# Ten pairs of channel blocks per layer of an input projection made from seven products of quarters instead of eight

## The chip, the cores and the metric

The kernel runs on one core of one Trainium2 chip. The metric is the time of one execution in device microseconds. A core has a matrix engine (PE), a vector engine (DVE), an activation engine (ACT), a general engine (POOL) and a queue engine (SP) that issues the transfers; each works through its own list of instructions in order and waits on semaphores that the others raise. PE writes its sums to PSUM, in banks of 128x512 words.

## What is computed

Two layers of a decoder trunk over 1024 tokens of width 1024. Cut to what matters here, one layer is:

```python
h = rms_norm(x, norm_g)
proj = h @ w_in
(q_lat, kv_lat, k_rope, g_mla,
 c_h, c_b, c_c, g_conv,
 s_q, s_k, s_v, g_swa) = jnp.split(proj, offsets, axis=-1)
y_mla = mla_mixer(q_lat, kv_lat, k_rope, ...) * jax.nn.silu(g_mla)
y_conv = c_b * causal_conv3(c_c * c_h, conv_w) * jax.nn.silu(g_conv)
y_swa = swa_mixer(s_q, s_k, s_v, ...) * jax.nn.silu(g_swa)
return x + jnp.concatenate([y_mla, y_conv, y_swa], axis=-1) @ w_out
```

Three mixers share one input projection `w_in` and one output projection `w_out`: latent attention (`mla`), a short convolution (`conv`) and window attention (`swa`). Each of `c_h`, `c_b`, `c_c` and the three gates `g_` is 512 channels wide, four blocks of 128. These 24 blocks are what the change is about.

## The kernel before

Every matrix product is made in float32 accuracy from two parts: a matrix is split into a rounded part (`hi`) and the rest (`lo`), and `mm3` gives three matmuls for each 128 rows of the sum: hi x hi, hi x lo, lo x hi. The normalised input stands in SBUF transposed, as `xh` and `xl`, for two halves of 512 tokens. A weight chunk comes by DMA into `wraw`; DVE casts it to `whi` (L151) and POOL subtracts to give `wlo` (L153).

A layer runs through these stages.
- **Window stage.** The window attention goes by blocks of 128 tokens. Beside each step, a list (`P1_FILL`) says how many units of the projection PE makes to fill its waits. First come 16 token-major units (`unit_b`, `unit_a`), then channel-major ones: `unit_u` makes `c_h` and `c_c` of a block, `unit_cb` makes `c_b`. Probabilities `pr` are scaled on POOL (L340) ahead of their transposition on PE (L350); `sy` are copies of the transposed ones (ACT L351, DVE L352).
- **Channel-major part.** The rest of the 24 blocks is made by `chan_mm`: for a block of 128 channels and 512 tokens, 8 rows of the sum x 3 matmuls of 128x512, so 24. Two blocks and two halves of the tokens, here called a pair, are 4 x 24 = 96 matmuls. The convolution runs on DVE (L487, L489), a gate is a SiLU on ACT (L400) and a multiplication on POOL (L401). Results stay in SBUF: `ycv` for the convolution, `osw` for the window group, `gm` for the latent group's gate.
- **Output projection of two groups.** `split_y` splits `ycv` and `osw` into `yh` (ACT, L516) and `yl` (DVE and POOL, L517); `unit_o` multiplies by `w_out`. The preparations of the latent attention are spread over these units by lists (`O_STARTS`).
- **Latent attention**, then the output projection of its group and the next layer's input.

Tiles come from pools with a fixed number of buffers (`big` has eight of 2 MB under one tag); whoever asks for a buffer waits until the last use of the one before is over. The order on each engine is that in which the program is written, except where the program asks for an instruction to be put after another.

Of the kernel before, what the change touches and what calls it, by code (L numbers as in the profile page):

```python
# [47 lines left out]
X_BEFORE, X_ALONE, X_FREE = 1, 7, 2  # first input tiles: before the weights, after them, of these without a unit  # L48
P1_ORDER = 'badfe'  # window attention, one step: score, project, transpose, fill, values
P1_FILL = ([0, 0, 2, 1, 0, 1, 1, 2, 1, 2, 0, 0, 2, 1, 0, 1, 0, 2, 0, 1],  # L50
           [2, 2, 2, 2, 0, 0, 3, 1, 2, 1, 1, 2, 0, 1, 0, 1, 1, 2, 3, 0])  # units of the projection beside each step, in the first layer and in the others
C1_STEP, G0_STEP = 3, 16  # steps at which later weights are fetched
O_STARTS = [0, 0, 0, 0, 0, 0, 0, 0, 0, 0, 0, 0, 0, 1, 0, 0, 0, 0, 2, 0, 2, 1, 2, 1, 1, 1, 3, 2, 0, 0, 0, 0]  # attention's preparations per output unit
O_LIGHT = [0, 0, 0, 0, 0, 0, 0, 0, 0, 0, 0, 0, 0, 0, 0, 0, 0, 0, 0, 0, 0, 0, 0, 0, 0, 0, 0, 0, 1, 1, 0, 2]  # attention units per output unit
O_PLAN, O_ALLOC, O_W0 = 28, 10, 7
A_ORDER = 'qk2srsT'  # attention, one step: scores (s), queries (q, r), keys (k, 2), the unit before (T)
A_UNITS = [[0, 3, 1], [0, 3, 0], [1, 0, 0], [0, 2, 0], [1, 0, 1], [0, 2, 1], [1, 1, 0], [1, 1, 1]]  # head pair, query blocks, head
# [11 lines left out]
def trunk(ctx, tc, x, norm_g, w_in, w_qb, w_kvb, w_out, c_gain, c_rope, c_idb, c_ali, out):  # L69
# [13 lines left out]
    wp = ctx.enter_context(tc.tile_pool(name="wp", bufs=2))  # L83
# [48 lines left out]
    x1p = dram.tile([S, D], F32, name="x1p")  # L132
    xmid = dram.tile([S, D], F32, name="xmid")

# [1 line left out]
    def load_w(parts, K, later=None, eng=None):  # L136
        """Two tiles hi, lo [P, K, W]; the pieces run now, or go to the list `later`."""
        W = sum(p.shape[2] for p in parts)
        hi = wp.tile([P, 8 * WMAX], FR, name="whi", tag="hi")[:, :K * W].rearrange("p (k w) -> p k w", k=K)
        lo = wp.tile([P, 8 * WMAX], FR, name="wlo", tag="lo")[:, :K * W].rearrange("p (k w) -> p k w", k=K)  # L140
        st = K // 4

        def piece(k):
            raw = wp.tile([P, 2 * WMAX], F32, name="wraw", tag="raw", bufs=3)
            raw = raw[:, :st * W].rearrange("p (k w) -> p k w", k=st)
            off = 0
            for p in parts:
                w = p.shape[2]
                nc.sync.dma_start(out=raw[:, :, off:off + w], in_=p[:, k:k + st, :])
                off += w  # L150
            v.tensor_copy(hi[:, k:k + st], raw)  # L151
            e = eng[k // st % 2] if isinstance(eng, tuple) else eng or g
            e.tensor_tensor(out=lo[:, k:k + st], in0=raw, in1=f32(hi[:, k:k + st]), op=ALU.subtract)  # L153
# [7 lines left out]
        return hi, lo  # L161
# [60 lines left out]
    for l in range(depth):  # L222
# [649 lines left out]
        for n in range(32):  # L872
# [12 lines left out]
            if lts:  # L885
                lts.pop(0)()
# [116 lines left out]
```

## Time and profile before

| what | value |
|---|---|
| runs | 1594.34, 1597.46, 1597.6 us |
| median | 1597.46 us |
| span of the profiled execution, first to last instruction | 1593.3 us |
| PE, DVE, POOL, ACT busy | 96%, 58%, 47%, 39% |
| window stage, first and second layer | 13 to 247 us, 812 to 1060 us |
| channel-major part | 247 to 459 us, 1060 to 1252 us |
| output projection, with the attention's preparation | 459 to 582 us, 1252 to 1376 us |

The profile records one execution; of that one the span is known, and the table's runs are others. Busy time counts an instruction from start to end; matmuls overlap, so the rate of PE is read from the distance between starts. Stages were cut where the lines of PE's timeline change, to a few microseconds.

### The profile page before, as it was taken

Reading aid. Unit: us, or ns where it says so; the run is one execution under the profiler, and the core shown is the slowest. Engines: PE = TensorE matmul, PEld = TensorE weight load, DVE = VectorE, ACT = ScalarE, POOL = GpSimd, SP = SyncE. Lnnn points to the kernel's source line nnn. Section 1 sums busy time; section 2 is a strip of 40 time slices with the busy share of each in tenths; the row PEclk is TensorE's granted clock in tenths of the full one; section 3 lists DMA queues with packets and bytes.
Section 4 is the critical chain, followed back from the end, with each engine's and each line's share of the span. In section 5 each row is a group of like instructions: output and inputs, shape, how many; then the busy total and the mean of one; then the engine's idle time right before and its main releaser. Section 6 shows DMA issues by size and latency. Waiting matters only on the chain. (4 is left out here: it accounts for less than half of the span.)

```text
span 1593.3 us, 25290 instructions
## 1 busy us (share of the span) xinstructions
PE 1521.6 (96%) x9276; PEld 1340.9 (84%) x9276; DVE 918.6 (58%) x1975; ACT 618.6 (39%) x1583; POOL 742.2 (47%) x976
## 2 busy tenths in 40 slices
PE   6999989999999999999989999989999999999998
PEld 5898868888889988878778988878888899888887
DVE  6676573232136668987656757643221455788864
ACT  4454441000130258985524444310001302688851
POOL 6444252233436646874244443433234466568640
PEclk9999999999999999999999999989999999999999
DMA  6101021122316410012241010121123163100123
GB/s 203 34 1 42 14 54 36 44 53 53 91 51 184 128 48 1 8 60 100 81 128 33 22 35 19 36 53 46 35 52 94 54 195 110 47 2 14 48 75 131
DMA packets 110461, 100.16 MB, mean 63 GB/s; under 512 B 16641, under 2 KB 102529, under 8 KB 110338
## 3 DMA queue, kind: packets, MB, share of 16 engines
q1 hardware_dynamic: 110338, 98.56, 21.0%
q8 instruction: 73, 1.20, 0.3%
q14 instruction: 50, 0.41, 0.1%
HBM read 81.76 MB, written 16.78 MB: 62 GB/s over the span
## 5 line engine op out<-in xcount | busy, mean ns | idle before, releaser
L153 POOL TENSOR_TENSOR wlo<-wraw,whi 128x512 fp32r<-128x512 f32 (+2 forms) x200 | 273.6, 1382 | 276.6 <-DVE whi L151 153.8
L166 PE MATMUL ps_g<-xh,whi 128*128 128x512 f32 x768 | 301.1, 392 | 3.4 <-DVE whi L151 2.2
L151 DVE CAST whi<-wraw 128x512 fp32r<-128x512 f32 (+2 forms) x208 | 136.5, 691 | 289.2 <-PE ps_g L167 199.8
L168 PE MATMUL ps_g<-xh,wlo 128*128 128x512 f32 x768 | 300.4, 391 | 0.3 <-POOL wlo L153 0.3
L167 PE MATMUL ps_g<-xl,whi 128*128 128x512 f32 x768 | 300.0, 391 | 0.0
L166 PEld LDWEIGHTS ps_g<-xh,whi 128*128 128x128 f32 x768 | 144.8, 189 | 34.3 <-issue 1.6
L168 PEld LDWEIGHTS ps_g<-xh,wlo 128*128 128x128 f32 x768 | 144.6, 188 | 30.9 <-POOL wlo L153 0.7
L167 PEld LDWEIGHTS ps_g<-xl,whi 128*128 128x128 f32 x768 | 144.8, 188 | 29.6
L166 PE MATMUL ps_g<-whi,xh 128*128 128x320 f32 (+2 forms) x512 | 157.9, 308 | 3.3 <-ACT xh L192 1.7
L167 PE MATMUL ps_g<-wlo,xh 128*128 128x320 f32 (+2 forms) x512 | 156.0, 305 | 1.7 <-POOL wlo L153 1.7
L168 PE MATMUL ps_g<-whi,xl 128*128 128x320 f32 (+2 forms) x512 | 156.7, 306 | 0.0
L166 PE MATMUL ps_g<-whi,yh 128*128 128x256 f32 x512 | 146.6, 286 | 0.3 <-DVE xr L533 0.3
L167 PE MATMUL ps_g<-wlo,yh 128*128 128x256 f32 x512 | 144.8, 283 | 0.0
L168 PE MATMUL ps_g<-whi,yl 128*128 128x256 f32 x512 | 144.8, 283 | 0.0
L774 PE MATMUL ps_g<-pt,vs 128*128 128x256 f32 (+1 forms) x640 | 120.6, 300 | 13.7 <-DVE pt L769 8.7
L400 ACT ACTIVATE gt<-ps_g 128x512 f32<-128x512 f32 x32 | 19.1, 598 | 250.8 <-PE ps_g L168 250.8
L774 PEld LDWEIGHTS ps_g<-pt,vs 128*128 128x128 f32 x640 | 91.4, 190 | 25.5 <-DVE pt L769 15.1
L769 DVE TENSOR_TENSOR pt<-ps_t,pt 128x512 fp32r<-128x512 f32 (+1 forms) x160 | 100.2, 632 | 16.2 <-ACT pt L768 14.3
L730 PE MATMUL ps_s<-kt,qh 96*128 96x512 f32 (+3 forms) x384 | 106.3, 361 | 1.0
L746 POOL TENSOR_SCALAR apr<-apr,ari 128x896 f32<-128x896 f32 (+2 forms) x80 | 71.7, 896 | 75.3 <-DVE ari L745 63.7
L340 POOL TENSOR_SCALAR pr<-pr,sri 128x256 f32<-128x256 f32 (+1 forms) x128 | 59.1, 480 | 99.7 <-DVE sri L338 62.4
L166 PEld LDWEIGHTS ps_g<-whi,xh 128*128 128x128 f32 x512 | 99.1, 194 | 5.0 <-ACT xh L192 2.3
(197 smaller groups left out, 3473.4 us busy)
## 6 DMA issues: line engine op xcount, KB each, us to landing
wraw<-in_w_out_dram SPq DMA_DIRECT2D x80, 256.0 KB, 3.1
wraw<-in_w_in_dram SPq DMA_DIRECT2D x144, 128.0 KB, 2.3
wraw<-in_w_in_dram SPq DMA_DIRECT2D x56, 256.0 KB, 2.8
x1p<-xr SPq DMA_DIRECT2D x16, 512.0 KB, 3.0
p<-x1p SPq DMA_DIRECT2D x16, 512.0 KB, 3.3
x<-in_x_dram SPq DMA_DIRECT2D x8, 512.0 KB, 4.5
xr<-in_x_dram SPq DMA_DIRECT2D x8, 512.0 KB, 5.3
xmid<-p SPq DMA_DIRECT2D x8, 512.0 KB, 2.8
```

What stands on the lines that cost most here:

```text
L151: v.tensor_copy(hi[:, k:k + st], raw)
L153: e.tensor_tensor(out=lo[:, k:k + st], in0=raw, in1=f32(hi[:, k:k + st]), op=ALU.subtract)
L166: pe.matmul(o, lhsT=lh, rhs=rh, start=(i == 0), stop=False)
L167: pe.matmul(o, lhsT=lh, rhs=rl, start=False, stop=False)
L168: pe.matmul(o, lhsT=ll, rhs=rh, start=False, stop=(i == n - 1))
L340: g.tensor_scalar(out=pr[:, h, k0:], in0=pr[:, h, k0:], scalar1=ri[:, h:h + 1], scalar2=1.0, op0=ALU.mult, op1=ALU.mult)
L400: s.activation(out=gt, in_=o, func=AF.Silu)
L730: pe.matmul(sp[:, kk], lhsT=a[:, hs], rhs=kt[0:QK, b, h, kk], start=(ai == 0), stop=(ai == 2 and c0 + w < n))
L746: g.tensor_scalar(out=pr[:, :n], in0=pr[:, :n], scalar1=ri, scalar2=1.0, op0=ALU.mult, op1=ALU.mult)
L769: v.tensor_tensor(out=pt[:, 1, lo_c:], in0=tp[:, lo_c:], in1=f32(pt[:, 0, lo_c:]), op=ALU.subtract)
L774: pe.matmul(av[:, q0:], lhsT=vb, rhs=pt[:, a, q * 256 + q0:(q + 1) * 256], start=(bb == 0 and bi == 0 and a == 0), stop=(last and bi == 1 ...
```

## The change

The kernel gets a second way to make a pair of blocks. The weights of two blocks of 128 channels are a matrix of two by two quarters (128 channels x 512 rows of the sum), the normalised input one of two by two quarters (512 rows x 512 tokens). Strassen's scheme in Winograd's form gives their product from seven products of quarters instead of eight, each of 4 x 3 = 12 matmuls, with sums of quarters before and after. Per layer:
- Only block 0 of the convolution (`c_h`, `c_c`, `c_b` and its gate) is still made by `chan_mm`, in the window stage and right after it. The other ten pairs go through `seven`, in the order u1, u2, g1, u3, g2, g3, s0, s1, m0, m1 (u: `c_h` and `c_c` of a block; g: `c_b` and the gate of the convolution; s, m: two blocks of the window group's and of the latent group's gate). The second layer's window stage has four units fewer to fill with: 22 instead of 26.
- Sums of the weights are made per pair in `quarters`: four on DVE, seven casts on ACT, the low parts three on DVE and four on POOL.
- Sums of the input's quarters are made once per layer: `t_one` makes T3 and T1 piece by piece in steps 9 to 12 and 14 to 17 of the window stage, `t_rest` makes T2 and then overwrites one quarter of the input itself by the fourth sum (T4), right before the pairs.
- Sums of products: products 1 and 2 gather in PSUM bank a, 6 and 7 in b, then 4 in b, and 5 and then 3 in c. Three banks hold a pair, and two pairs have a set each. ACT copies product 1 (`s1`); DVE makes `s2`, `s3` and the three `plus`, each of which frees a bank for the product behind it.
- SBUF is short for this, so the latents, the window group's output, the convolution's results and the latent group's gate are written to DRAM and read back later. The weight buffers become eight small ones for `hi` and for `lo`. `split_y` moves ahead of the end of this stage, since its inputs come back from DRAM. Three numbers delay the preparation of the latent attention (`O_LAT`, `O_GMR`, `O_ALLOC`).

The core of the diff:

```diff
+        def t_diff(k, tmp, a, b, e):
+            d = tmp()
+            e[0].tensor_tensor(out=d, in0=f32(a[0][:, k]), in1=f32(b[0][:, k]), op=ALU.subtract)
+            e[1].tensor_tensor(out=d, in0=d, in1=f32(a[1][:, k]), op=ALU.add)
+            e[2].tensor_tensor(out=d, in0=d, in1=f32(b[1][:, k]), op=ALU.subtract)
+            return d
...
+        def t_one(n, k):
+            a, b, e = {1: (quarter(0, 1), quarter(0, 0), (g, v, g)), 3: (quarter(1, 1), quarter(0, 1), (g, v, g))}[n]
+            t_split(k, t_diff(k, raw_tile, a, b, e), TT[n][:, 0], TT[n][:, 1])
+
+        def t_rest(k, tmp):
+            f = t_diff(k, tmp, quarter(1, 1), (TT[1][:, 0], TT[1][:, 1]), (v, g, v))
+            t_split(k, f, TT[2][:, 0], TT[2][:, 1])
+            for i in range(2):
+                (v, g)[i].tensor_tensor(out=f, in0=f32(quarter(1, 0)[i][:, k]), in1=f, op=ALU.subtract if i == 0 else ALU.add)
+            t_split(k, f, *quarter(0, 1))
...
+            for n, first in ((3, T_STEPS[0]), (1, T_STEPS[1])):
+                if i == first:
+                    t_alloc(n)
+                if first <= i < first + 4:
+                    with tc.issue_after(marks["exp"].ins):
+                        t_one(n, i - first)
...
+            def split(n, a, e):
+                h, lo = (t.rearrange("p (k c) -> p k c", k=4) for t in w_pair(512))
+                s.copy(out=h, in_=a)
+                e.tensor_tensor(out=lo, in0=a, in1=f32(h), op=ALU.subtract)
...
+            v.tensor_tensor(out=t, in0=a21, in1=a22, op=ALU.add)
+            split(1, a11, g)
+            split(5, t, g)
+            v.tensor_tensor(out=a21, in0=a11, in1=a21, op=ALU.subtract)
+            v.tensor_tensor(out=t, in0=t, in1=a11, op=ALU.subtract)
+            split(6, t, v)
+            split(7, a21, v)
+            split(2, a12, g)
+            v.tensor_tensor(out=t, in0=a12, in1=t, op=ALU.subtract)
+            split(4, a22, g)
+            split(3, t, v)
...
+            a, b, c = ps_c()
+            product(a, 1, True)
+            s1 = st()
+            s.copy(out=s1, in_=a)
+            if first:
+                product(c, 5, True)
+                product(a, 2, False)
+                c11(a)
+            product(b, 6, True)
+            s2 = st()
+            v.tensor_tensor(out=s2, in0=b, in1=s1, op=ALU.add)
+            if not first:
+                product(c, 5, True)
+            product(b, 7, False)
+            s3 = st()
+            v.tensor_tensor(out=s3, in0=b, in1=s1, op=ALU.add)
+            if not first:
+                product(a, 2, False)
+                c11(a)
+            c22(c, s3)
+            product(b, 4, False)
+            c21(b, s1)
+            product(c, 3, False)
+            c12(c, s2)
...
+        w = quarters(O_CH + P, O_CC + P)
+        for k in range(4):
+            t_rest(k, st)
+        osw = a16("osw", F32).rearrange("p (k q) -> p k q", k=4)
+        nc.sync.dma_start(out=osw, in_=osw_d)
+        group_u(1, w)
+        for f, j in ((group_u, 2), (group_g, 1), (group_u, 3), (group_g, 2), (group_g, 3),
+                     (group_s, 0), (group_s, 1), (group_m, 0), (group_m, 1)):
+            f(j)
```

How this changes the order on two engines is shown at two places of the first layer. The names are those of the program with a running number: `st` is a scratch tile, `xh` and `xl` the input's parts, `asum`, `a12` and `wraw` sums or raw weights of a pair.

**POOL at the start of the channel-major part, before.** The rows begin behind the last scaling of probabilities; `ycv` times `gt` is the first block's gate.
```order
L153 TENSOR_TENSOR wlo_2841<-wraw_2842,whi_2840 128x512 [waits DMAHW3_49,DMAHW4_49,DVE_49,PE_49]
L153 TENSOR_TENSOR wlo_2841<-wraw_2847,whi_2840 128x512 [waits DMAHW6_49,DMAHW5_49,DVE_49]
L153 TENSOR_TENSOR wlo_2841<-wraw_2852,whi_2840 128x512 [waits DMAHW7_49,DMAHW0_49,DVE_49]
L153 TENSOR_TENSOR wlo_2841<-wraw_2857,whi_2840 128x512 [waits DMAHW2_49,DMAHW1_49,DVE_49]
L401 TENSOR_TENSOR ycv_2775<-ycv_2775,gt_2809 128x512 [waits DVE_49,Activation_49]
L153 TENSOR_TENSOR wlo_2977<-wraw_2978,whi_2976 128x512 [waits DMAHW3_49,DMAHW4_49,DVE_49,PE_49]
L153 TENSOR_TENSOR wlo_2977<-wraw_2983,whi_2976 128x512 [waits DMAHW6_49,DMAHW5_49,DVE_49]
L401 TENSOR_TENSOR ycv_2775<-ycv_2775,gt_2837 128x512 [waits Activation_49]
```

**POOL at the same place, now.** The first two rows are the last two gate multiplications of block 0.
```order
L537 TENSOR_TENSOR u_2587<-u_2587,ch_2762 128x512 [waits Activation_49]
L537 TENSOR_TENSOR u_2587<-u_2587,ch_2791 128x512 [waits Activation_49]
L472 TENSOR_TENSOR st_2870<-st_2870,xl_331 128x512 [waits DVE_49]
L570 TENSOR_TENSOR wlo_2844<-asum_2837,whi_2843 128x512 [waits Activation_49]
L401 MEMSET u_3010 128x2 [waits DMAHW7_49,DMAHW0_49,Pool_49]
L472 TENSOR_TENSOR st_2880<-st_2880,xl_331 128x512 [waits DVE_49,PE_49]
L472 TENSOR_TENSOR st_2890<-st_2890,xl_331 128x512 [waits DVE_49]
L472 TENSOR_TENSOR st_2900<-st_2900,xl_331 128x512 [waits DVE_49]
L570 TENSOR_TENSOR wlo_2858<-a12_2835,whi_2857 128x512 [waits DMAHW1_49,PE_49,Activation_49]
L570 TENSOR_TENSOR wlo_2863<-wraw_2833,whi_2862 128x512 [waits DMAHW3_49,PE_49,Activation_49]
L487 TENSOR_TENSOR st_2870<-xl_191,st_2870 128x512 [waits DVE_49]
L466 TENSOR_TENSOR T2_2828<-st_2880,T2_2828 128x512 [waits Activation_49]
```

Between the last gate and the low parts of the first pair's weights (`wlo_2844` for product 5, `wlo_2858` for product 2) there now stand sums for T2 and T4 (L472, L487), and eight further rows, sums or low parts, follow until T4's last low part.

**DVE at the end of the channel-major part, before.** The output projection's weights, and the first half of `split_y`.
```order
L151 CAST whi_4017<-wraw_4031 128x512 [waits DMAHW2_49]
L517 TENSOR_TENSOR yl_4036<-ycv_2775,yh_4035 128x512 [waits PE_49,Activation_49]
L517 TENSOR_TENSOR yl_4036<-ycv_2775,yh_4035 128x512 [waits Activation_49] x2
L517 TENSOR_TENSOR yl_4036<-osw_100,yh_4035 128x512 [waits Activation_49] x2
L517 TENSOR_TENSOR yl_4036<-osw_100,yh_4035 128x512 [waits Activation_49,Pool_49]
L151 CAST whi_4140<-wraw_4142 128x512 [waits DMAHW3_49,PE_49,Pool_49]
L151 CAST whi_4140<-wraw_4146 128x512 [waits DMAHW4_49]
```

**DVE at the same place, now.** The second half of `split_y` (L702) stands between the sums of the last pair's products; `ps_c_4214` is the last pair's PSUM, `st` its sums.
```order
L702 TENSOR_TENSOR yl_4346<-yv_4347,yh_4345 128x512 [waits DMAHW1_49,PE_49,Activation_49]
L702 TENSOR_TENSOR yl_4346<-yv_4351,yh_4345 128x512 [waits DMAHW2_49,Activation_49]
L702 TENSOR_TENSOR yl_4346<-yv_4355,yh_4345 128x512 [waits DMAHW4_49,Activation_49]
L702 TENSOR_TENSOR yl_4346<-osw_2910,yh_4345 128x512 [waits Activation_49]
L627 TENSOR_TENSOR st_4267<-ps_c_4214,st_4267 128x512 [waits Activation_49]
L702 TENSOR_TENSOR yl_4346<-osw_2910,yh_4345 128x512 [waits Activation_49]
L702 TENSOR_TENSOR yl_4346<-osw_2910,yh_4345 128x512 [waits Activation_49,Pool_49]
L173 CAST whi_4479<-wraw_4478 128x512 [waits DMAHW6_49,PE_49,Pool_49]
L627 TENSOR_TENSOR st_4227<-ps_c_4214,st_4227 128x512 [waits PE_49]
L173 CAST whi_4485<-wraw_4484 128x512 [waits DMAHW0_49,PE_49]
L627 TENSOR_TENSOR st_4241<-ps_c_4214,st_4241 128x512 [waits PE_49]
```

The `plus` of L627 that frees a bank for product 4 now stands behind four low parts of `yl`, each of which waits for a cast on ACT.

## Rows read from the trace of the kernel before

**Rows 1.** The page's head: busy time and share of the span of each engine.
```profile
span 1593.3 us, 25290 instructions
...
PE 1521.6 (96%) x9276; PEld 1340.9 (84%) x9276; DVE 918.6 (58%) x1975; ACT 618.6 (39%) x1583; POOL 742.2 (47%) x976
```

**Rows 2.** By stage: stretch, length, busy PE, PEld, DVE, ACT, POOL, granted clock, DMA share, GB/s.
```profile
13.00:247.00 234.00, 215.11 (x1394) 193.78 (x1395) 157.92 (x396) 104.85 (x326) 108.44 (x166) 1.00 0.16 43
247.00:459.00 212.00, 212.00 (x937) 175.54 (x936) 53.60 (x70) 16.94 (x28) 74.28 (x57) 1.00 0.22 58
...
812.00:1060.00 248.00, 231.60 (x1439) 210.85 (x1438) 153.24 (x392) 95.05 (x311) 102.60 (x159) 0.96 0.15 38
1060.00:1252.00 192.00, 192.00 (x848) 158.99 (x848) 48.39 (x63) 18.12 (x31) 68.72 (x53) 1.00 0.22 58
```

**Rows 3.** Timeline of PE: start, length; the second row is twelve matmuls after the first.
```profile
439.68 0.39 PE L166 MATMUL ps_g<-xh,whi 128*128 128x512 f32 x1
...
442.40 0.39 PE L166 MATMUL ps_g<-xh,whi 128*128 128x512 f32 x1
```

**Rows 4.** PE's waits by releaser: us in total, times, longest us.
```profile
PE ps_t L350 <- POOL pr L340: 9.9, 6, 4.2
...
PE ps_g L360 <- ACT sy L351: 7.6, 14, 0.6
```

**Rows 5.** Groups by line and shape: busy us, mean ns of one, idle before and releaser.
```profile
L489 DVE SCALAR_TENSOR_TENSOR ycv<-u,gains,ycv 128x512 f32<-128x512 f32 x24 | 21.9, 918 | 0.6
...
L401 POOL TENSOR_TENSOR osw<-osw,gt 128x512 f32<-128x512 f32 x16 | 20.6, 1284 | 28.9 <-ACT gt L400 28.9
...
L400 ACT ACTIVATE gt<-ps_g 128x512 f32<-128x512 f32 x32 | 19.1, 598 | 250.8 <-PE ps_g L168 250.8
...
L516 ACT CAST yh<-ycv 128x512 fp32r<-128x512 f32 x16 | 8.7, 618 | 18.5 <-PE ps_g L167 18.5
...
L388 DVE TENSOR_TENSOR u<-ps_g,ch 128x512 f32<-128x512 f32 x12 | 8.2, 686 | 20.7 <-PE ps_g L168 20.7
...
L487 DVE TENSOR_SCALAR ycv<-u,gains 128x512 f32<-128x512 f32 x12 | 7.3, 621 | 0.4
```

**Rows 6.** Timelines of DVE and then POOL from 453 to 478 us: start, length, count.
```profile
471.75 5.18 DVE L517 TENSOR_TENSOR yl<-ycv,yh 128x512 fp32r<-128x512 f32 x3
...
477.19 0.68 DVE L517 TENSOR_TENSOR yl<-osw,yh 128x512 fp32r<-128x512 f32 x1
...
453.25 1.29 POOL L153 TENSOR_TENSOR wlo<-wraw,whi 128x512 fp32r<-128x512 f32 x1 [0.80 <-DVE whi L151]
...
470.19 4.50 POOL L153 TENSOR_TENSOR wlo<-wraw,whi 128x512 fp32r<-128x512 f32 x3 [4.88 <-PE ps_g L168]
474.64 1.74 POOL L517 TENSOR_TENSOR yl<-ycv,yh 128x512 fp32r<-128x512 f32 x1
```

**Rows 7.** Timeline of PE around 1050 us in the second layer's window stage.
```profile
1047.27 0.69 PE L350 MATMUL ps_t<-idn,pr 128*128 128x128 f32 x2 [4.19 <-POOL pr L340]
...
1051.20 0.63 PE L166 MATMUL ps_g<-xh,whi 128*128 128x512 f32 x1
1051.62 0.63 PE L167 MATMUL ps_g<-xl,whi 128*128 128x512 f32 x1
...
1055.46 0.41 PE L167 MATMUL ps_g<-xl,whi 128*128 128x512 f32 x1
```

**Rows 8.** Stretches around the same place, columns as in rows 2.
```profile
1047.00:1052.00 5.00, 4.22 (x15) 3.59 (x16) 2.09 (x4) 1.07 (x2) 1.57 (x4) 0.50 0.01 2
1052.00:1056.00 4.00, 4.00 (x12) 3.09 (x11) 0.00 (x0) 0.00 (x0) 0.00 (x0) 0.57 0.00 0
1056.00:1060.00 4.00, 4.00 (x19) 3.30 (x18) 0.33 (x1) 1.07 (x3) 0.00 (x0) 1.00 0.00 0
```

**Rows 9.** DMA issues: KB each, median us from issue to landing.
```profile
wraw<-in_w_in_dram SPq DMA_DIRECT2D x144, 128.0 KB, 2.3
```

More of the change, by code (lines that the diff above doesn't have):

```diff
@@ L1 @@
-from contextlib import ExitStack
+from contextlib import ExitStack, nullcontext
 import numpy as np
@@ new lines, in seven, with product @@
+        def seven(c1, c2, c11, c21, c22, c12, w=None):
+            first = w is not None
+            w = w or quarters(c1, c2)
+            def product(o, n, first):
+                (ah, al), (bh, bl) = w[n], qx[n]
+                for k in range(4):
+                    for i, (a, b) in enumerate(((ah, bh), (ah, bl), (al, bh))):
+                        pe.matmul(o, lhsT=a[:, k], rhs=b[:, k], start=(first and k == 0 and i == 0),
+                                  stop=(k == 3 and i == 2), skip_group_check=True)
+            a, b, c = ps_c()
[22 more added lines that the diff above has]
+            c12(c, s2)
@@ new lines, in plus, with silu, group_u @@
+        def plus(o, a):
+            v.tensor_tensor(out=a, in0=o, in1=a, op=ALU.add)
+            return a
+        def silu(o, a=None):
+            r = st() if a is None else plus(o, a)
+            s.activation(out=r, in_=o if a is None else r, func=AF.Silu)
+            return r
+        def group_u(j, w=None):
+            u_tile(j)
+            got = {}
+            seven(O_CH + j * P, O_CC + j * P, lambda o: got.update(a=o),
+                  lambda o, a: v.tensor_tensor(out=uu[j][:, 2:514], in0=got["a"], in1=plus(o, a), op=ALU.mult),
+                  lambda o, a: got.update(d=plus(o, a)),
+                  lambda o, a: g.tensor_tensor(out=uu[j][:, 514:1026], in0=plus(o, a), in1=got["d"], op=ALU.mult), w)
@@ new lines, in group_g, with times, store, last @@
+        def group_g(j):
+            yv = [cp.tile([P, 512], F32, name="yv", tag="yv", bufs=3) for _ in range(2)]
+            for hf in range(2):
+                conv(j, hf, yv[hf])
+            def times(hf, a, e):
+                e.tensor_tensor(out=yv[hf], in0=a, in1=yv[hf], op=ALU.mult)
+            def store(hf):
+                nc.sync.dma_start(out=ycv_d[:, j, hf * 512:hf * 512 + 512], in_=yv[hf])
+            def last(o, a):
+                times(1, plus(o, a), g)
+                store(1)
+            def c21(o, a):
+                times(0, silu(o, a), g)
+                store(0)
+            seven(O_CB + j * P, O_GC + j * P, lambda o: times(0, o, v), c21, lambda o, a: times(1, silu(o, a), g), last)
```

244 lines of the change are left out of this document (148 added, 96 removed).

## The prediction

> **What bounds the kernel now.** I read the page's busy times first: PE is busy 96% of the span and no other engine is above 58% [rows 1]. Because such a share averages unlike stages, I then cut the span at the stages. In the channel-major part PE never stops (212.00 of 212.00 us in the first layer, 192.00 of 192.00 in the second), while DVE, ACT and POOL have 53.60, 16.94 and 74.28 us of work in the first [rows 2]. So there the time is the number of matmuls times the distance between their starts. In the two window stages PE stands still for 18.9 and 16.4 us [rows 2], most of it behind POOL's normalisation `pr` (9.9 us) and ACT's copies `sy` (7.6 us) [rows 4].
>
> The distance is read from starts, not from the 0.39 us of one row, since matmuls overlap: twelve 128x512 matmuls lie between 439.68 and 442.40 us [rows 3], so 2.72 / 12 = 0.2267 us each.
>
> **What is removed.** A pair of blocks takes 7 x 12 = 84 matmuls instead of 4 x 24 = 96, for ten pairs in each of two layers: 240 matmuls, 54.4 us, or 27.2 per layer. They come out of a stage where nothing else limits, so this is lost only to new waits. Those follow, per layer.
>
> **Start of the pairs.** Before, POOL had four low parts of weights per four units here. Now its queue holds, behind the last gate's multiplication, 17 operations of 128x512 up to the last low part of the fourth token quarter, and PE needs that after 82 matmuls (six products and ten more), 18.6 us of work. POOL starts them 2.2 us after the last gate unit ends: the SiLU takes 0.60, the multiplication 1.29 [rows 5], the handovers some 0.3. One operation takes POOL 1.29 alone and DVE 0.68 alone; where both run such operations the trace shows both slow: three of DVE in 5.18 us while POOL goes from three in 4.50 to one in 1.74 [rows 6], so one of each in 1.73 us. DVE's queue here has as many two-input operations, so I take 1.73 for all: 2.2 + 17 x 1.73 = 31.6, minus 18.6, gives 13.0 us of stall. It comes in pieces: product 5 waits for the second of the 17, product 2 for the sixth (until 12.6, PE being ready at 8.4: 4.2 us), product 6 for the ninth and tenth, product 4 for the last two. If they do not hinder one another it is 2.2 + 17 x 1.29 - 18.6 = 5.5. One after the other, 1.29 + 0.68 = 1.97 gives 17.1.
>
> That pair of rows is where a rule bears on the change. The Trainium skill (SBUF — State Buffer, Who interferes with whom) says that a DVE operation with two SBUF inputs and a GpSimd operation that reads SBUF take a shared port pair as an exclusive lock, the second one standing still until the first is through. That is the 1.97: 4.1 us more per layer, and about 1615 in all. The trace agrees that they hinder one another, not that nothing overlaps (1.73, not 1.97).
>
> **End of the pairs.** The last pair has no partner whose products could fill its waits, and before this end had no wait at all. Product 2 waits for `s3` (an eviction from PSUM, 0.69 [rows 5], with handovers 0.9). Product 4 waits for the `plus` that frees its bank, and that stands on DVE behind four `yl` of `split_y(1)`, each waiting for a cast on ACT; the casts start when product 2 ends, because `yh` takes a buffer of the normalised input. So 4 x 0.62 [rows 5] + 0.7 + 0.69 = 3.9 us. Product 3 waits for the next `plus`: 0.7 to 1.3. With a slowed `yl` among them I take 7 (5 to 9).
>
> **Clock.** After PE's 4.19 us gap the granted clock is 0.50 to 0.57 until about 1055 us, that is 1.2 instead of 2.4 GHz, and two matmuls are 0.42 apart instead of 0.23 [rows 7, 8]; the ten from 1051.20 to 1055.46 took 2.0 us too long. My chains hold two gaps of about that size per layer. At the start POOL sets the pace, so a slower PE hides; at the end it does not. I take 2 (0 to 4, both or none).
>
> **Steady pairs.** In three pairs (the second gate pair `s` and both `m`) product 1 of the next pair but one comes one matmul behind product 3, and waits for that bank's `plus`: 0.8 each, 2.4 in all. A pair gives PE 84 x 0.2267 = 19.0 us. In a pair of the convolution's gate DVE has seven weight operations (1.73 each beside POOL, 0.68 alone), two convolutions (four `scalar_tensor_tensor` at 0.92 and two scalings at 0.62 [rows 5]), five evictions and a multiplication (0.69 each): 12.1 + 4.9 + 4.1 = 21.1 us, or 13.8 alone. Fully hindered, three such pairs are late by 6.3. I take 5, between 2 (the handovers alone) and 9.
>
> **Window stage.** Its last steps get 20 POOL operations (26 us), 12 on DVE and 8 casts for two token quarters. The second subtraction of a piece waits on POOL for DVE, and the next `pr` stands behind it, which PE already waits for. Projection units beside it can hide that: then nothing. If half of POOL's time shows, 14 (with one more DVE wait). The 16 to 19 us that PE now loses in a whole stage are nearer to the low end; I take 5, some 0.6 for each of eight pieces.
>
> **Transfers.** Spills and reloads of the latents, the window output, the convolution and the last gate are (1.7 + 3 x 2.1) MB, twice, in two layers: 32 MB. In the pairs the DMA engines are busy for 0.22 now [rows 2], and a 128 KB weight load lands in 2.3 us [rows 9], well ahead of its pair. I take nothing; if the 2 MB reload ahead of the second pair's weights showed, it would hide under the start's stall.
>
> **Sum per layer.** 13.0 + 7 + 2 + 5 + 5 = 32.0 of new waiting against 27.2 saved: 4.8 slower, 9.6 for both. The profiled span is 1593.3; the median of the runs, 1597.46, stands 4.2 above it, which I add: 1593.3 + 9.6 + 4.2 = 1607.1. All low ends (12.5) give 14.7 faster per layer, 1568; all high ends (53) 25.8 slower, 1649.
>
> **Rivals.** (a) *Faster, about 1579*: DVE and POOL hinder each other little, since their queues rarely meet (in the pairs now POOL is busy for 74 of 212 us, DVE for 54). Then the start costs 5.5, the steady pairs 2.4, the window 3, the end 7 and the clock nothing: 17.9 instead of 32, 9.3 faster per layer. The point that decides is how long one of the 17 operations takes: with all else as forecast the sum crosses zero when the start costs 8.2, that is at (8.2 + 18.6 - 2.2) / 17 = 1.45 us. Against it: where the trace has both queues full, none ran at its own pace [rows 6].
> (b) *Clean gain, 1543 to 1560*: PE's sequence is held up only at the end. That needs the token sums before the pairs, and the order of POOL's queue puts 17 of its operations behind the last gate.
> (c) *Much slower, about 1633*: the window's `pr` waits for the whole of a token piece (14 per layer) and the three gate pairs are late on DVE throughout (9): 13 + 7 + 2 + 9 + 14 = 45, 17.8 per layer. For it: `pr` is already PE's longest wait there; against: projection units are left in those steps.
> (d) *No change*: the terms cancel within measurement.
> That the matmuls are not saved is no rival: the program holds 240 fewer of the same shape.
>
> **Chances.** The measurement can tell 0.2% (3.2 us) from no change. The forecast case, slower up to 1625, has 0.34; (c), above that, 0.15; (d) 0.12; (a), 1562 to 1594, 0.31; (b) 0.08. So faster 0.39, same 0.12, slower 0.49. The low end of the range leaves out (b), the high end the worst part of (c): 1562 to 1640. Within the forecast's own case it is 1600 to 1625.
>
> **What would show it.** In the profile after: PE with idle stretches summing to 10 to 14 us in the 32 us behind the last gate unit, released by POOL's `wlo`, `T2` and `xl`; DVE's and POOL's sums of 128x512 at 1.3 to 1.8 us where they meet; at the end of the pairs a gap of about 4 us before product 4, released by DVE, and lower clock right behind it; between, PE over 95% busy; window stages longer by some 5 us. I am wrong if POOL's 17 take under 26 us, if the end's casts are there earlier, or if the window stages do not lengthen.

## The result and the profile after

The changed kernel takes 1648.2 us (median; 1646.07 to 1649.39), the kernel before 1597.53 us in the same comparison: ratio 1.0325, 95% interval 1.0306 to 1.0344. The forecast was 1607 with a range to 1640: the direction was right, the size was not, and the time is outside the range. The profiled span is 1647.3 us.

The page's head, beside [rows 1]: 240 matmuls are gone, and PE is busy for 16 us less in a span that is 54 us longer.

```profile
span 1647.3 us, 25601 instructions
...
PE 1505.8 (91%) x9036; PEld 1315.3 (80%) x9036; DVE 1102.5 (67%) x2179; ACT 725.9 (44%) x1763; POOL 856.3 (52%) x1050
```

The windows of the changed kernel in its first layer (columns as in [rows 2]): window stage, start of the pairs, middle, last hundred us.

```profile
13.00:264.30 251.30, 226.09 (x1412) 204.42 (x1412) 174.51 (x409) 112.41 (x337) 133.31 (x182) 0.96 0.18 53
264.30:300.00 35.70, 23.36 (x80) 16.64 (x81) 28.46 (x25) 11.36 (x21) 27.88 (x19) 0.86 0.34 105
300.00:400.00 100.00, 97.91 (x423) 80.00 (x422) 61.46 (x87) 28.50 (x49) 42.53 (x32) 0.98 0.27 72
400.00:499.60 99.60, 84.41 (x341) 66.31 (x340) 52.16 (x62) 32.90 (x57) 47.62 (x34) 0.93 0.35 108
```

Where PE never stopped before [rows 2], it now makes 80 matmuls in 35.7 us and 341 in 99.6, and the clock is down. The middle is nearly full. I call *lost* the length of a stretch less its matmuls, each at the median distance between starts of its form. By this count the pairs lose in the two layers 18.6 and 19.5 us at the start (17.8 and 18.5 of it from their first matmul on, by which the experiments are counted), 4.4 and 2.6 in the middle and 22.6 and 20.5 in the last hundred us; the window stage loses 11.9 and 8.0 more than before (the second counted, in both kernels, from the first matmul of its layer). That is 54.1 per layer on average; less the 27.2 saved, 26.9, and the spans differ by 54.0 / 2 = 27.0.

PE's waits in the changed kernel by releaser (us in total, times, longest), beside [rows 4]. L598 is a matmul of a product, L604 the copy `s1`, L611 `s2`, L616 `s3`, L627 `plus`; `pr`, L340 before, is L365.

```profile
PE ps_t L375 <- POOL pr L365: 17.4, 10, 3.6
PE ps_c L598 <- DVE st L627: 14.6, 10, 4.5
PE ps_c L598 <- DVE st L611: 13.5, 2, 6.8
PE ps_c L598 <- DVE st L616: 10.9, 4, 3.6
PE ps_c L598 <- ACT st L604: 10.1, 8, 1.5
PE ps_g L385 <- ACT sy L376: 8.9, 15, 0.8
...
PE ps_c L598 <- POOL wlo L570: 4.2, 2, 2.1
```

POOL's low parts, on which the forecast put the start's stall, release 4.2 us here. DVE's sums of products and ACT's copies of product 1 release 49. The two longest are `s2`, once per layer. PE's timeline at the start (start, length, and at the end of a row the idle time ahead and its releaser):

```profile
274.95 0.80 PE L598 MATMUL ps_c<-xh,wlo 128*128 128x512 f32 x1 [2.07 <-POOL wlo L570]
...
291.60 1.22 PE L598 MATMUL ps_c<-T,whi 128*128 128x512 f32 x2 [6.76 <-DVE st L611]
```

DVE in the same stretch:

```profile
282.84 1.77 DVE L487 TENSOR_TENSOR st<-xh,st 128x512 f32<-128x512 f32 x1
...
285.13 1.74 DVE L487 TENSOR_TENSOR st<-xh,st 128x512 f32<-128x512 f32 x1
286.80 1.75 DVE L575 TENSOR_TENSOR asum<-wraw 128x512 f32<-128x512 f32 x1
288.46 1.76 DVE L487 TENSOR_TENSOR st<-xh,st 128x512 f32<-128x512 f32 x1
290.15 0.68 DVE L578 TENSOR_TENSOR wraw<-wraw 128x512 f32<-128x512 f32 x1
290.85 0.69 DVE L611 TENSOR_TENSOR st<-ps_c,st 128x512 f32<-128x512 f32 x1
```

`s2` itself takes 0.69 us. PE had stopped at 284.8 with all of product 6 issued, and `s2` began 6.0 us later; it stood behind the sums for T4 and for the next pair's weights, at 1.75 each beside POOL.

PE's timeline in the last hundred us:

```profile
412.49 0.47 PE L598 MATMUL ps_c<-xh,whi 128*128 128x512 f32 x1 [0.65 <-DVE st L627]
...
419.65 0.74 PE L598 MATMUL ps_c<-T,whi 128*128 128x512 f32 x2 [1.45 <-ACT st L604]
...
480.54 0.80 PE L598 MATMUL ps_c<-xh,whi 128*128 128x512 f32 x1 [3.60 <-DVE st L616]
...
490.53 0.79 PE L598 MATMUL ps_c<-xh,whi 128*128 128x512 f32 x1 [4.50 <-DVE st L627]
...
496.80 0.51 PE L598 MATMUL ps_c<-xh,whi 128*128 128x512 f32 x1 [0.78 <-DVE st L627]
```

The second row is odd: it is product 6, the first into bank b, and it waits for ACT's copy `s1`, which reads bank *a*. The first two waits come three times per layer, 2.1 us each time. Ahead of the third, DVE has six low parts of `split_y(0)` in front of `s3`:

```profile
471.66 4.08 DVE L702 TENSOR_TENSOR yl<-yv,yh 128x512 fp32r<-128x512 f32 x3
475.66 2.95 DVE L702 TENSOR_TENSOR yl<-osw,yh 128x512 fp32r<-128x512 f32 x3
...
479.81 0.68 DVE L616 TENSOR_TENSOR st<-ps_c,st 128x512 f32<-128x512 f32 x1
```

The clock in windows around the start's gap (columns as in [rows 2], the granted clock third from the end):

```profile
288.00:292.00 4.00, 0.40 (x1) 0.40 (x2) 3.97 (x5) 1.76 (x4) 3.37 (x3) 0.53 0.00 0
292.00:296.00 4.00, 4.00 (x12) 3.13 (x12) 0.50 (x1) 0.60 (x1) 4.00 (x3) 0.61 0.02 4
```

And in windows behind the two longer gaps of the end:

```profile
480.50:485.00 4.50, 4.46 (x11) 3.51 (x12) 0.00 (x0) 0.05 (x1) 1.15 (x1) 0.50 0.92 335
...
490.50:495.00 4.50, 4.47 (x11) 3.51 (x12) 1.86 (x2) 1.25 (x2) 2.27 (x2) 0.50 0.49 176
```

Eleven matmuls take the 4.5 us in which twenty would fit. Added up over stretches of 2 us, the time at 1.2 GHz is 23 us in the kernel before and 103 us now.

One sentence ahead of the prediction has to be put right: the order on each engine is not simply that of the program's text. In the trace, products of two pairs stand mixed on PE, and `split_y`'s low parts (L702), written behind the last pair, run on DVE ahead of its evictions.

### The profile page after: what moved, and what is told of

Read it like the earlier page. It is cut to its first block, busy times and chain, and to the rows that moved or that the text cites. A ratio compares the mean times of both kernels' runs of the same rounds, so it can differ in the third digit from the quotient of the medians.

```text
span 1647.3 us, 25601 instructions
## 1 busy us (share of the span) xinstructions
PE 1505.8 (91%) x9036; PEld 1315.3 (80%) x9036; DVE 1102.5 (67%) x2179; ACT 725.9 (44%) x1763; POOL 856.3 (52%) x1050
## 5 line engine op out<-in xcount | busy, mean ns | idle before, releaser
L175 POOL TENSOR_TENSOR wlo<-wraw,whi 128x512 fp32r<-128x512 f32 (+2 forms) x120 | 165.7, 1388 | 136.3 <-DVE whi L173 113.0
L598 PE MATMUL ps_c<-T,whi 128*128 128x512 f32 x480 | 155.2, 403 | 26.5 <-DVE st L611 13.5
L598 PE MATMUL ps_c<-xh,whi 128*128 128x512 f32 x320 | 131.2, 410 | 30.0 <-DVE st L627 14.6
L598 PEld LDWEIGHTS ps_c<-T,whi 128*128 128x128 f32 x480 | 91.8, 193 | 52.7 <-DVE st L611 14.4
L598 PE MATMUL ps_c<-xh,wlo 128*128 128x512 f32 x320 | 129.5, 405 | 4.2 <-POOL wlo L570 4.2
L598 PE MATMUL ps_c<-xl,whi 128*128 128x512 f32 x320 | 129.0, 403 | 0.0
L173 DVE CAST whi<-wraw 128x512 fp32r<-128x512 f32 (+2 forms) x128 | 76.8, 609 | 62.5 <-DMA wraw<-in_w_out_dram 20.6
L598 PEld LDWEIGHTS ps_c<-xh,whi 128*128 128x128 f32 x320 | 62.4, 195 | 52.5 <-DVE st L627 13.3
L932 DVE TENSOR_REDUCE am<-ps_s 128x1 f32<-128x128 f32 (+7 forms) x128 | 95.6, 750 | 9.2 <-PE ps_s L930 7.1
L966 ACT CAST pt<-ps_t 128x512 fp32r<-128x512 f32 (+1 forms) x160 | 85.7, 543 | 35.2 <-PE ps_g L192 17.9
```

The source lines that it names most:

```text
L173: v.tensor_copy(hi, raw)
L175: e.tensor_tensor(out=lo, in0=raw, in1=f32(hi), op=ALU.subtract)
L598: pe.matmul(o, lhsT=a[:, k], rhs=b[:, k], start=(first and k == 0 and i == 0), stop=(k == 3 and i == 2), skip_group_check=True)
L932: v.tensor_reduce(out=m, in_=sp[:, :n], axis=AX.X, op=ALU.max)
L966: s.copy(out=pt[:, 0, lo_c:], in_=tp[:, lo_c:])
```

## The experiments

Ratios are to the kernel before, with 95% intervals; the changed kernel is 1.0325. "Lost" is given for the first layer / the second.

### One suspect at a time

**`split_y`'s low parts moved off DVE.**
```diff
-                (g if k % 4 >= 3 else v).tensor_tensor(out=yl[:, k], in0=src, in1=f32(yh[:, k]), op=ALU.subtract)
+                g.tensor_tensor(out=yl[:, k], in0=src, in1=f32(yh[:, k]), op=ALU.subtract)
```


> All low parts of split_y go to POOL instead of three quarters of them to DVE; nothing else changes. Theory (the end of the pairs is slow because the evictions that free a bank stand on DVE behind split_y's low parts, and the gaps of 3.60 and 4.50 us that this makes lower the clock): the two gaps shrink to about 1 us each, the low clock at 480 to 495 us goes, some 2.7 + 3.5 + 4.8 = 11 us per layer, so about 1626 in place of 1648. Rival (the last pair has no partner, so its chain of evictions and the reloads from DRAM are slow in themselves): the gaps stay within 1 us of what they were, 1644 to 1650.

Measured: 1641.36 us, 1.0283 (1.0263 to 1.0304). The gaps of 3.60 and 4.50 became 1.46 and 3.26, the one of 0.78 became 2.53. The end lost 19.0 / 16.3 instead of 22.6 / 20.5: the queue on DVE is part of it, the smaller part.

**Without T2 and T4.**
```diff
-            f = t_diff(k, tmp, quarter(1, 1), (TT[1][:, 0], TT[1][:, 1]), (v, g, v))
...
+                s.copy(out=TT[2][:, i, k], in_=f32(TT[1][:, i, k]))
```


> The sums T2 and T4 right before the pairs are left out: T2 is filled by eight copies on ACT and the overwritten quarter stays as it is, so the products of these quarters are those of other numbers. Theory (the start of the pairs waits for DVE's and POOL's queues of these sums): of 18.6 us lost there some 15 come back in each layer, about 1618. Rival (the first pair's weights, their transfers and their own low parts hold the start): at most 5 per layer come back, 1638 or more.

Measured: 1633.34, 1.0236 (1.0216 to 1.0255). The start lost 7.8 / 7.8 instead of about 18: ten of it belong to these sums, less than the theory said.

**Without T1 and T3.**
```diff
-            t_split(k, t_diff(k, raw_tile, a, b, e), TT[n][:, 0], TT[n][:, 1])
+            for i in range(2):
+                s.copy(out=TT[n][:, i, k], in_=f32(a[i][:, k]))
```


> The sums T1 and T3 in the window stage are left out: both are filled by copies on ACT of one quarter instead of 20 operations on POOL, 12 on DVE and 8 casts per layer. Theory (these operations stand ahead of the scaling of probabilities): PE's loss in the window stages falls from 53.5 and 39.5 us to the 41.6 and 30.2 of before, so 21 us, about 1627. Rival (the loss comes from the other order of the fill units, the later weights and the spills): the loss stays above 48 and 36, 1640 or more.

Measured: 1644.98, 1.0314 (1.0295 to 1.0332). The window stage lost 7.8 / 6.1 less, but the middle of the pairs 3.0 / 6.6 more, so that the end time hardly moved.

**PE kept at work in the waits**, by 24 matmuls into a spare bank ahead of product 7 of the first pair, and 14 and 16 ahead of products 2 and 4 of the last.
```diff
+                for i in range(n):
+                    r = pe.matmul(f, lhsT=k[0], rhs=k[1], start=(i == 0), stop=(i == n - 1), skip_group_check=True)
```


> Matmuls into a spare bank that nothing reads are put into three waits of PE per layer: 24 before product 7 of the first pair, 14 before product 2 and 16 before product 4 of the last. They are shorter than the gaps that they stand in (5.4 of 6.8, 3.2 of 3.6, 3.6 of 4.5 us at full clock). Theory (the half clock after these gaps costs some 2 us at the start and 5 to 6 at the end of each layer's pairs): clock 1.00 there and 8 us less per layer, about 1633. Rival (the half clock does not come from PE's idleness, or costs nothing since other engines set the pace): within 3 us of 1648, or slower.

Measured: 1645.2, 1.0313 (1.0289 to 1.0338). Time at 1.2 GHz fell from 103 to 68 us. At the end, with the fillers counted as lost, the loss fell by 4.1 / 1.7 us: there the low clock has a price of its own. At the start nothing was won, but this does not show that the clock costs nothing there: product 7 began at 292.60 at full clock, and then, with four operations on weights now ahead of `s3` and `plus` on DVE, PE met a wait that the changed kernel does not have, with lower clock behind it (0.81 from 300.9 to 310).

```profile
301.81 0.50 PE L609 MATMUL ps_c<-xh,whi 128*128 128x512 f32 x1 [3.92 <-DVE st L644]
```

**All low parts of `split_y` on POOL as above, and all of `split_y(1)` behind the last SiLU.**
```diff
+        with tc.issue_after(marks["silu"].ins):
+            split_y(1)
-        split_y(1)
```


> As the first experiment (all low parts of split_y on POOL), and the casts of split_y's second half on ACT are put behind the last pair's last SiLU. The first experiment left gaps of 1.46, 3.26 and 2.53 us: the plus before product 4 now waited for a SiLU that stands on ACT behind four of these casts. Theory (at the end of the pairs PE waits for whatever stands ahead of the evictions, on DVE and on ACT): the gap of 3.26 falls to about 1.5 and the low clock there goes, 3 to 4 us more per layer than in the first experiment, ratio 1.023 against its 1.028. Rival (the last pair's chain is that long in itself): the ratio stays at 1.028.

Measured: 1652.83, 1.035 (1.0316 to 1.0383), slower. PE's timeline at the end:

```profile
483.82 0.50 PE L598 MATMUL ps_c<-xh,whi 128*128 128x512 f32 x1 [1.46 <-DVE st L627]
...
491.05 0.80 PE L598 MATMUL ps_c<-xh,whi 128*128 128x512 f32 x1 [4.22 <-DVE st L627]
```

The wait ahead of product 4 went from 4.50 to 1.46, as meant, but product 3 now waits 4.22, and the output projection loses 8.1 / 10.4 instead of 1.4 / 2.2. The work was put off, not hidden.

**u1 made by `chan_mm`**, four units beside T2 and T4, so nine pairs.
```diff
+            s.copy(out=ch, in_=chan_mm(W["u1"], 0, hf))
+            v.tensor_tensor(out=uu[1][:, 2 + hf * 512:514 + hf * 512], in0=chan_mm(W["u1"], P, hf), in1=ch, op=ALU.mult)
...
-        group_u(1, w)
```


> The pair u1 is made by four plain units again, 96 matmuls instead of 84, right after the window stage and its first units; the sums T2 and T4 run beside it. Nine pairs are left. Theory (the start waits for the queues of these sums, which the plain units cover for 21.8 us): of 18.6 us lost at the start some 4 stay, against 2.7 us of matmuls given back, so 12 per layer, ratio 1.018. Rival (whichever pair comes first stalls, since its weights come late and its own evictions stand behind sums on DVE): at least 12 us stay lost, ratio above 1.028.

Measured: 1640.66, 1.0275 (1.0238 to 1.0312). The start of the pairs lost 3.9 / 3.7, but the stall had moved ahead of it:

```profile
292.84 0.77 PE L597 MATMUL ps_c<-xh,whi 128*128 128x512 f32 x1 [7.31 <-DVE u L682]
```

The plain units' own evictions stand behind T2's and T4's sums on DVE.

**T2 and T4 on DVE alone, T1 and T3 on DVE alone** (two kernels).
```diff
-            f = t_diff(k, tmp, quarter(1, 1), (TT[1][:, 0], TT[1][:, 1]), (v, g, v))
+            f = t_diff(k, tmp, quarter(1, 1), (TT[1][:, 0], TT[1][:, 1]), (v, v, v))
```


> The sums T2 and T4 run on DVE alone: its queue at the start gets 12 operations more, POOL's 12 fewer, nothing is left out. Theory (a two-input operation takes 0.68 us on DVE alone and 1.75 beside one on POOL, so sharing this work between them buys nothing): DVE's 35 operations take about 35 x 0.68 + 5 x 1.05 = 29 us instead of 33 for its present share, and the start loses 4 us less per layer: ratio 1.027. Rival (DVE's operations take 1.1 us on average for other reasons, so 12 more of them take 13 us more): the start loses 9 us or more in addition, ratio above 1.043.

> The sums T1 and T3 in the window stage run on DVE alone; POOL loses 20 operations per layer there and DVE gets them, nothing is left out. Theory (the scaling of probabilities on POOL stands behind these sums): PE's wait for it, 17.4 us now and 9.9 in the kernel before, falls to about 11, ratio 1.028. Rival (any 32 operations more in these steps are too many, and DVE has the longer queue): the wait moves to DVE's copies and evictions, ratio 1.033 or more.

Measured: 1647.34, 1.0322 (1.0295 to 1.0349), and 1650.35, 1.0338 (1.0312 to 1.0364). In the first the start lost 15.1 / 15.8, 2.7 less, though DVE had twelve operations more per layer: most now run at 0.60 to 0.69, since POOL is mostly idle, so two engines that take 1.75 each beside one another gain little here over one. What was won there was lost again elsewhere, most of it in the middle. In the second the waits for `pr` fell from 17.4 to 13.0, and 12.9 of waits for scores on ACT stand beside them, 3.9 before. Which of the two engines makes the sums is not what matters.

### The cause at the end: one PSUM tile for three banks

The odd wait of product 6 for a reader of bank a suggested that waits are kept for a whole tile, and `ps_c` is one tile of three banks.
```diff
-        t = pp["pool"].tile([P, 3 * 512], F32, name="ps_c", tag="C", bufs=2)
-        return [t[:, i * 512:i * 512 + 512] for i in range(3)]
+        return [pp["pool"].tile([P, 512], F32, name=f"ps_c{n}", tag=f"C{n}", bufs=2) for n in "abc"]
```


> The three PSUM banks of a pair become three tiles of their own, so that a product waits only for the eviction of its own bank; in the changed kernel one tile holds all three, and a product waits for the last reader of any of them. Theory (at the end and between the last pairs PE waits for evictions of other banks: 0.65 us before product 1 of the next pair but one, 1.45 before product 6, 4.5 before product 4): the three handovers of 2.1 us go, and product 4 waits for s3 alone; some 10 us less wait and 2 us less of low clock per layer, ratio 1.0175 against 1.0325. Rival (the waits are for the data, whose evictions are queued behind other work on DVE and ACT): the waits only move to the next product, ratio above 1.028.

Measured: 1611.34, 1.0098 (1.0079 to 1.0117). This edit of one function, with the same operations, gives back 36.9 us, more than expected. The windows of the start and the middle: the middle is full, 441 matmuls in 99.5 us, and the start is as it was, 18.2 / 18.9.

```profile
265.00:300.50 35.50, 24.81 (x78) 17.01 (x78) 28.43 (x26) 10.36 (x18) 27.96 (x19) 0.81 0.35 111
300.50:400.00 99.50, 99.50 (x441) 82.39 (x440) 68.77 (x90) 30.56 (x52) 48.85 (x33) 1.00 0.26 71
```

Only what PE waits for at the start has changed: `s2` now holds it for 1.12, and a cast of the next pair's weights for 4.40. That cast waits on ACT for DVE's sum of these weights, which stands in the same queue behind the sums for T4.

```profile
292.00 1.22 PE L597 MATMUL ps_cc<-T,whi 128*128 128x512 f32 x2 [4.40 <-ACT whi L568]
```

The end loses 4.5 / 4.5. Its one gap on PE's timeline stands ahead of product 4:

```profile
472.17 0.79 PE L597 MATMUL ps_cb<-xh,whi 128*128 128x512 f32 x1 [2.68 <-DVE st L615]
```

**On that base: u1 by `chan_mm`, and with it the low parts of `split_y` on POOL** (edits as above).

> As the one before, and the pair u1 by four plain units beside the sums T2 and T4. Theory (start and end are separate losses): the 0.5% that the plain pair gave alone adds up, ratio 1.0125. Rival (a stall saved at the start comes back at the end, since the evictions set the pace of all pairs): as without it, 1.0175 or more.

> As the one before, and all low parts of split_y on POOL. Theory (s3 of the last pair still stands behind these on DVE): the 0.4% that this gave alone adds up, ratio 1.008 or 1.009. Rival (with a bank of its own for each product the queue no longer holds PE, and POOL delays the output weights instead): ratio 1.0125 or more.

Measured: 1599.65, 1.0024 (1.001 to 1.0038), and 1611.18, 1.0105 (1.009 to 1.012). The first gains more than its theory said; the second falls between theory and rival. In it the end loses nothing, and the output projection 12.8 / 12.5. PE's wait there is not for `yl` itself but for `xr`, the eviction that adds the layer's input, whose transfer SP issues behind transfers that wait 5.0 for POOL's `yl` and 2.8 for POOL's `wlo`. The waits of PE and of SP's queue in the first layer, from 471 us:

```profile
PE ps_g L189 <- DVE xr L734: 6.9, 1, 6.9
...
SPq L798 <- POOL yl L705: 5.0, 1, 5.0
SPq L150 <- POOL wlo L174: 2.8, 2, 2.0
```

### The start: order or amount

On the kernel with three PSUM tiles and u1 by `chan_mm`: **T4's sums put behind the plain units' last eviction**, and then **`split_y(0)` behind the `plus` that follows the last pair's `s3`**, and then that **without T1 and T3**.
```diff
+        with tc.issue_after(mul.ins):
+            for k in range(4):
+                t_four(k, fs[k])
...
+        with tc.issue_after(marks["c22"].ins):
+            split_y(0)
```


> As the run with a tile per bank and u1 by plain units; in addition DVE's operations for the fourth token quarter T4 are put behind the eviction of the last plain unit. That run still waited at the start, in one layer 7.2 and in the other 4.6 us, for this eviction, which stood on DVE behind the sums. Theory (the order on DVE, not its amount of work, makes this wait): the waits fall to about 1 us, 5 per layer, ratio 0.996 against 1.0024. Rival (the sums are late anyway and product 4 of the first pair then waits for T4): ratio 1.001 or more.

> As the one before, and DVE's low parts of split_y's first half are put behind the last pair's s3 and the plus that frees the third bank. Theory (product 4 of the last pair waits 2.7 us for s3 behind them, and the clock falls after it): some 4 us more per layer, ratio 0.991. Rival (the output projection then waits for these low parts instead): ratio equal to the one before.

> As the one before, with the sums T1 and T3 of the window stage left out and filled by copies on ACT. In the changed kernel this gave 7 us per layer back in the window stages, and 3 to 7 of them were lost again in the pairs. Theory (those were waits for other banks, and the sums cost 7 us per layer in the window stage): ratio lower by 0.009 than the one before. Rival (the time saved in the window stage returns in the pairs for another reason): lower by at most 0.004.

Measured: 1598.26, 1.0023 (1.001 to 1.0036); 1604.37, 1.0066 (1.0043 to 1.0089); 1592.07, 0.998 (0.9966 to 0.9993). In the first the wait for the eviction is gone and another has come:

```profile
303.95 1.22 PE L599 MATMUL ps_cb<-T,whi 128*128 128x512 f32 x2 [4.75 <-DVE st L612]
```

Both orders cost the same, so it is the amount of sums in this place, not their order. In the second the end lost 1.1 / 0.9 and the output projection 8.8 / 9.4, the third edit by which `yl` comes later and is paid for there. The third prices T1 and T3 at 0.0086 of the time, about 7 us per layer.

### The sums made by PE

The sums of the input's quarters are linear, so PE can make them by matmuls with plus or minus the identity: four of 128x512 per piece, 0.9 us, then a cast on ACT and one subtraction on DVE, in place of three sums (two for T4), a cast and a low part that DVE, POOL and ACT share. First T2 and T4, on the kernel with three PSUM tiles and all ten pairs; then T1 and T3 too.
```diff
+        def t_pe(k, a, b, h, lo):
+            o = ps_g()
+            for i in range(4):
+                pe.matmul(o, lhsT=eye[:, i // 2], rhs=(a, b)[i // 2][i % 2][:, k], start=(i == 0), stop=(i == 3))
+            s.copy(out=h[:, k], in_=o)
+            v.tensor_tensor(out=lo[:, k], in0=o, in1=f32(h[:, k]), op=ALU.subtract)
```


> Three PSUM tiles for the three banks, and the sums T2 and T4 of the input's quarters, at the start of the pairs, are made by PE: per slice four matmuls of 128x512 with plus or minus the identity, then a cast on ACT and one subtraction on DVE. All ten pairs and the whole computation are kept. It adds 32 matmuls, 7.3 us, per layer. Theory (the start is lost to the sums' queue on DVE and POOL): the start, 18.2 and 18.9 us lost with three PSUM tiles, falls to about 10 per layer, 7.3 of it the new matmuls; the rest unchanged: ratio 1.000 (0.996 to 1.004) to the kernel before, 1595 us. Rival (PE still waits for the cast and the subtraction of each slice in turn, some 1.3 us per slice): the start costs as much as with the sums on DVE and POOL, ratio 1.008 to 1.012.

> As the kernel with T2 and T4 made on PE, and T1 and T3, in the window stages, too; a scratch tile of the attention's output has one buffer instead of two to make room. The whole computation is kept. 32 more matmuls, 7.3 us, per layer, in a stage where PE has waits. Theory: the window stage loses its 7 us per layer of waits that leaving T1 and T3 out had shown, and half of the new matmuls lie in PE's own waits: 3 us better per layer than the kernel with T2 and T4 alone, ratio 0.997 (0.993 to 1.001). Rival (the new matmuls show in full, and PE waits for the casts on ACT, which the window's softmax uses too): no gain or worse, ratio 1.000 to 1.006.

Measured: 1588.8, 0.996 (0.9947 to 0.9972), and 1580.46, 0.9916 (0.9901 to 0.9931). Both are faster than the kernel before, each at the good end of its theory or beyond it. The page's head of the second:

```profile
span 1578.0 us, 25771 instructions
...
PE 1499.9 (95%) x9164; PEld 1324.2 (84%) x9164; DVE 1064.7 (67%) x2163; ACT 723.1 (46%) x1763; POOL 765.0 (48%) x986
```

The windows of its starts of the pairs:

```profile
258.00:293.70 35.70, 35.70 (x159) 29.57 (x158) 23.23 (x33) 15.78 (x28) 14.09 (x11) 1.00 0.47 145
...
1041.00:1077.00 36.00, 36.00 (x161) 29.81 (x160) 23.07 (x33) 15.97 (x28) 13.95 (x11) 1.00 0.48 146
```

Its PE's waits for `pr`:

```profile
PE ps_t L377 <- POOL pr L367: 6.0, 5, 2.2
```

The start of the pairs, 80 matmuls in 35.7 us in the changed kernel, holds 159 here at full clock, 32 of them for the sums (7.3 us, about the 7.8 that the start still lost when T2 and T4 were left out): PE works through other products while a piece is cast, so the serial wait that the rival counted does not show. In the window stage the waits for `pr` fall from 17.4 to 6.0 us, and with the clock's share the stage loses 13.3 / 10.6 less than in the changed kernel, its new matmuls not counted. The time at 1.2 GHz is 34 us. Against the changed kernel the losses fall by 23.9 in the window stages, 36.3 at the starts, 7.4 in the middles and 35.8 at the ends, and rise by 5.0 in the output projections: 98.4, less 128 matmuls at 0.2267, 29.0, is 69.4, and the spans differ by 69.3.

## Why the prediction was wrong

The sum was 32.0 us of new waiting per layer; it was 54.1. The saving of 27.2 holds. Term by term, as means of the two layers:

| term | forecast | measured |
|---|---|---|
| start of the pairs | 13.0 (5.5 to 17.1) | 19.0 |
| end of the pairs, with the clock | 7 + 2 | 15.2 |
| steady pairs | 5 (2 to 9) | 3.5 in the middle + 6.3 in handovers = 9.8 |
| window stage | 5 (0 to 14) | 10.0 |
| transfers | 0 | no wait of PE's above is released by one |

**End and steady pairs: the step that failed.** These terms are half of the 22 us by which the sum was short (the start is 6, the window stage 5). The prediction let each product wait for the eviction "that frees its bank". What PE waited for was the last reader of any of the three banks, because they are one tile. That puts a handover of 2.1 us between products three times per layer, where I had 0.8 each. Product 2's wait for `s3` was in the sum, at 0.9; it was 3.60, since I had not seen that `s3` reads another bank than the one that product 2 writes, nor that six low parts of `split_y(0)` stand ahead of it on DVE. The 4.50 ahead of product 4 and the 0.78 ahead of product 3 are what was worked out (3.9 and 0.7 to 1.3). With a tile for each bank the end and the steady pairs together cost 4.4 instead of 25.0 per layer. The program's order had shown one name, `ps_c_4214`, on all three `plus`; I had read it as three.

**Start.** The end of POOL's queue was right, in part by luck: its last low part ends at 296.1 us, 32.5 behind the last gate unit, forecast 31.6, but the 17 operations took 1.57 on average, not 1.73, and POOL stood idle between them for 3.8. DVE and POOL slow each other as [rows 6] had it: 1.75 and 1.71 where they meet, 0.68 and 1.29 apart. Here the Trainium skill's rule of the lock (SBUF — State Buffer, Who interferes with whom) would give, as an estimate, 1.97 for the pair of operations; the trace again shows less. Wrong was that PE would have made its 82 matmuls when POOL is done. It was held before, by `s2` on DVE behind T4's sums (6.76), which is in none of the four pieces that the prediction lists. So DVE's queue, not POOL's, held PE there, by `s2` in this kernel and by the next pair's weights in the one with three tiles; the sums on DVE alone (15.1) and the two orders agree with that, and the sums on PE, which end it, show that it was this work in this place. POOL has its part in that queue's slowness (1.75 beside it, 0.68 without).

**Window stage.** PE's waits grew by 5.7 / 3.5, near the 5 taken, but the mechanism named, `pr` behind the sums on POOL, accounts for that in the first layer alone. The waits for `pr` up to the pairs, before and then now, first layer and then second:

```profile
PE ps_t L350 <- POOL pr L340: 3.7, 3, 2.5
PE ps_t L375 <- POOL pr L365: 10.5, 7, 3.3
...
PE ps_t L350 <- POOL pr L340: 6.3, 3, 4.2
PE ps_t L375 <- POOL pr L365: 6.9, 3, 3.6
```

In the second layer waits for DVE and ACT grew instead, such as those for the normalised input (`p` at L205, 3.8 to 5.4) and for the softmax on ACT (none to 1.8); what delays them was not tested. Without T1 and T3 the waits for `pr` are 6.3 / 3.9 instead of 10.5 / 6.9, so the sums do hold it up in both layers, but in the second by hardly more than it was held up before. The prediction also called the waits for `pr` and `sy` most of PE's standing still before; 17.5 of 35.3 is half. The rest, up to 10.0, is matmuls at 1.2 GHz (4.6 / 2.7 more than before) and gaps too short to be listed.

**Clock.** I allowed 2 us, at the end alone. Matmuls at half rate cost 4.7 / 2.9 there and 4.6 / 2.7 more in the window stage. That it hides at the start, as the prediction held, is not shown, since the run with fillers met another wait there.

The kernel with three PSUM tiles, 1611.3, comes close to the 1607.1 forecast, but not by the forecast's terms: its start and window cost more and its end less. Rival (c), 1633, was the nearest in time, by a `pr` later than it was (14 per layer) and gate pairs late on DVE, which they were not: the middle is full once the tile is split. The point that decides rival (a), POOL's operations at 1.45 us, was not reached (1.57). Two costs stay open: I did not try another place for `split_y` that makes `yl` neither late nor in the way, and the last gap ahead of product 4 (2.68) is still there in the fastest kernel.

## What to carry to other kernels

Count, for each bank that a product goes to, who else reads the tile it belongs to: here one tile over three banks made products wait for evictions of the other two, and splitting the tile cost nothing and gave 37 us. When a scheme saves matmuls by sums on other engines, follow the evictions that stand in the same queue as the sums, not the sums alone; if the sums are linear, a few matmuls with an identity may be cheaper than the queue (128 of them, 29 us of PE's time, left the kernel 31 us faster). Work moved to a later place has to be looked for there: three of these edits to `split_y` gained at the end of the pairs and lost more than that in the output projection.

## What the runs showed of the hardware

The clock fell behind gaps shorter than the 4.19 us of [rows 7]: after 3.60 us PE was granted 0.50 for 4.5 us, and time at 1.2 GHz grew from 23 to 103 us. No simple rule can be read from the gaps. In the kernel with all sums on PE the wait ahead of product 4 is 2.68 us in both layers, behind pairs in which PE had not waited once, and the clock behind it differs (columns as in [rows 2], first layer and then second):

```profile
453.00:457.00 4.00, 3.71 (x16) 3.09 (x17) 3.97 (x6) 3.28 (x7) 2.68 (x2) 1.00 0.89 360
...
1237.00:1241.00 4.00, 4.00 (x12) 3.12 (x11) 4.00 (x6) 2.56 (x5) 2.05 (x2) 0.57 0.92 360
```

In the kernel with three PSUM tiles the same wait of 2.68 us was followed by 4 us at 0.57. Fillers in such waits won back 4.1 / 1.7 us of the 4.7 / 2.9 that the half rate had cost at the end.
